# Activations in one tile per block of 512 tokens, and the last gate tiles block by block

## The chip, the cores and the metric

The kernel runs on one core of a Trainium2 chip. The metric is the time of one launch on the device in microseconds, here the median of three runs. Every matmul, vector operation and transfer that is named below belongs to that one core.

## The reference

Two layers of a hybrid encoder work on `x` of 2048 tokens and 1024 channels, in float32. What matters here:

```python
for l in range(DEPTH):                       # 2
    h = rms_norm(x, norm_w[l])
    proj = h @ w_in                          # q,k,v | z_a | decay, beta | conformer | gates
    q, k, v = silu(conv5(qkv)); q, k = l2_normalize(q), l2_normalize(k)
    o = delta_rule(q, k, v, g, beta) forwards + the same backwards, in chunks of tokens
    o = rms_norm per head(o) * dn_norm_w * silu(z_a)
    y_a = o @ w_dn_out
    u = silu(layer_norm(conv31(cf_val * sigmoid(cf_glu)))) * silu(z_b)
    y_b = u @ w_cf_out
    gate = sigmoid(gate_lg + gate_b)         # 2 x 1024 channels
    x = x + (gate[0] * y_a + gate[1] * y_b) @ w_out
return rms_norm(x, final_norm_w)
```

## The kernel before, in words

**Splits.** Each float32 operand of a dense product is split into a high part (`split`: a copy on ACT that rounds) and a low part (a subtraction on DVE). A dense product is three matmuls for every 128 input channels: high by high, high by low, low by high, each 128x512. In what follows a *unit* is three such matmuls. Weights come by `weight`: a load into `wraw` on SP's queue, then `whi` on ACT and `wlo` on DVE, with two buffers each.

**Stages of a layer.** First the projections, with conv, normalising and scalar work pumped in between. The last projection is the 16 tiles of gate logits (`gates`): half 0 (tokens 0 to 1023) runs there; half 1 is left as filling for the next stage. Then `delta`, 16 steps of the chunked delta rule, one chunk forwards (lane 0) and one backwards (lane 1) in each step. Then `merge`, which makes `y_a`, `y_b`, the gates and the product with `w_out`.

**One step of delta.** On TensorE: for both lanes `pk` (L971) and `pq` (L974), products of the keys and queries with the state; the next chunk's inverse is assembled in between by `prep` (L918, L928 and L931, L942 and L943, L951 and L952); `pw` (L987); `pn` and `po` (L996, L1005), the state's update and the output. From step 8 on a pair of chunks is ready in each step, and `finish` normalises it: squares on ACT (L1026), an rsqrt on DVE (L189 to L1040), scaling on ACT (L1044), transposes on TensorE (L1049), the product with `za` on DVE (L1050) and the store of `og`. These are short dependent pieces, so between them the program pulls filling: `pull(n)` takes n units from `filler`, and in each full step 5, 4, 4 and 4 of them. `pull` ends early at a `yield GAP`.

**The filling.** `filler` runs `gates(1)`, 32 products of 8 units, and then `early_merge`: it loads `u` of half 0 into the tile `uop`, splits it, and makes 16 products of 4 units into the tile `t1`. The order of PE, ACT, DVE and POOL in this stage is the written order (`bind`); SP's queue is ordered by a scheduler. The large tiles share four buffers. Activations `h` are kept as a high and a low tile per half, so half 1 holds two buffers up to the last unit of `gates(1)`; `uop` and `t1` need just these. So `early_merge` yields GAP eight times, four behind the loads and four with the splits: counted from 0, step 12 gets 12 units, 13 none and 14 eight, and what isn't pulled by the last step, 30 units, runs behind the last transposes. There, in `merge`, `og` is read back as `gop` and split, and its products with `w_dn` begin.

In `merge` the gate logits come back from memory as `gt` (L1206, a sigmoid on ACT), in buffers of the kind `hm`, five of them, which the rings of `delta` use too. `prep` loads the decay's rows as `gc` into the ring `rgb` (POOL adds a mask, L889, ACT takes the exponent, L895).

## Time and profile before

| | |
|---|---|
| median of 3 runs | 3243.44 us (3238.36 to 3246.26) |
| profiled execution | 3243.9 us |
| its span on the core | 3242.1 us |
| mean granted clock of TensorE | 0.986 |
| TensorE busy | 96 % |
| VectorE (DVE) busy | 74 % |
| ScalarE (ACT) busy | 43 % |
| GpSimd (POOL) busy | 9 % |

In the profile PE is TensorE, SP the queue that issues most transfers. A line such as L971 is one of the kernel before; in the changed kernel the same code stands four lines earlier in this stage (L967). A number in brackets is the time for which the engine stood idle ahead of the instruction, with what released it. The two layers have the same order; all rows are from the first, unless said.

### The profile page before, as it was taken

Reading aid. Unit: us, or ns where it says so; the run is one execution under the profiler, and the core shown is the slowest. Engines: PE = TensorE matmul, PEld = TensorE weight load, DVE = VectorE, ACT = ScalarE, POOL = GpSimd, SP = SyncE. Lnnn points to the kernel's source line nnn. Section 1 sums busy time; section 2 is a strip of 40 time slices with the busy share of each in tenths; the row PEclk is TensorE's granted clock in tenths of the full one; section 3 lists DMA queues with packets and bytes.
Section 4 is the critical chain, followed back from the end, with each engine's and each line's share of the span. In section 5 each row is a group of like instructions: output and inputs, shape, how many; then the busy total and the mean of one; then the engine's idle time right before and its main releaser. Section 6 shows DMA issues by size and latency. Waiting matters only on the chain. (4 is left out here: it accounts for less than half of the span.)

```text
span 3242.1 us, 51095 instructions
## 1 busy us (share of the span) xinstructions
PE 3110.2 (96%) x19110; PEld 2719.2 (84%) x19110; DVE 2392.3 (74%) x4401; ACT 1397.2 (43%) x3100; POOL 303.1 (9%) x297
## 2 busy tenths in 40 slices
PE   6999999999999998999999999999999999898998
PEld 5788888888878997787888888888887899887786
DVE  7689898997546687645676989898954567857655
ACT  5625152523344466533345242434234545655332
POOL 3000000000022231000000000000002122300000
PEclk9999999999999998999999999999999999999999
DMA  4323231324587786654413141313457777846634
GB/s 139 90 92 103 74 113 64 116 102 146 189 272 244 255 258 193 178 190 130 141 49 107 65 124 56 121 62 115 139 180 247 237 257 249 272 139 199 205 126 150
DMA packets 425879, 501.68 MB, mean 155 GB/s; under 512 B 95584, under 2 KB 260064, under 8 KB 425632
## 3 DMA queue, kind: packets, MB, share of 16 engines
q1 hardware_dynamic: 352880, 388.58, 38.6%
q10 hardware_dynamic: 64688, 80.09, 7.0%
q0 software_dynamic: 8064, 29.76, 2.4%
q8 instruction: 150, 2.46, 0.3%
q14 instruction: 97, 0.79, 0.1%
HBM read 342.74 MB, written 155.58 MB: 154 GB/s over the span
## 5 line engine op out<-in xcount | busy, mean ns | idle before, releaser
L173 PE MATMUL pd<-hhi,whi 128*128 128x512 f32 x2816 | 1093.8, 389 | 0.0
L175 PE MATMUL pd<-hhi,wlo 128*128 128x512 f32 x2816 | 1072.5, 381 | 2.0 <-DVE wlo L157 2.0
L174 PE MATMUL pd<-hlo,whi 128*128 128x512 f32 x2816 | 1073.2, 381 | 0.0
L734 DVE SCALAR_TENSOR_TENSOR cacc<-gp,vec,cacc 128x1009 f32<-128x1009 f32 (+1 forms) x480 | 614.2, 1280 | 38.0 <-ACT cacc L732 34.8
L173 PEld LDWEIGHTS pd<-hhi,whi 128*128 128x128 f32 x2816 | 535.6, 190 | 79.6 <-issue 1.2
L175 PEld LDWEIGHTS pd<-hhi,wlo 128*128 128x128 f32 x2816 | 535.1, 190 | 79.8 <-DVE wlo L157 3.6
L174 PEld LDWEIGHTS pd<-hlo,whi 128*128 128x128 f32 x2816 | 535.7, 190 | 73.1 <-issue 1.9
L156 ACT ACTIVATE whi<-wraw 128x512 fp32r<-128x512 f32 x400 | 242.9, 624 | 491.7 <-PE pd L174 337.0
L157 DVE TENSOR_TENSOR wlo<-wraw,whi 128x512 fp32r<-128x512 f32 x400 | 290.0, 738 | 217.6 <-ACT whi L156 207.9
L559 DVE SCALAR_TENSOR_TENSOR acc<-cin,vec,acc 128x1022 f32<-128x1022 f32 (+1 forms) x192 | 246.5, 1298 | 14.6 <-ACT acc L557 13.4
L175 PE MATMUL pd<-yhi,wlo 128*128 128x512 f32 x512 | 195.4, 382 | 5.9 <-DVE wlo L157 5.7
L173 PE MATMUL pd<-yhi,whi 128*128 128x512 f32 x512 | 195.2, 381 | 3.0 <-ACT whi L156 2.7
L174 PE MATMUL pd<-ylo,whi 128*128 128x512 f32 x512 | 194.3, 379 | 1.7 <-DVE ylo L157 1.7
L812 ACT ACTIVATE go<-pd,vec 128x512 f32<-128x512 f32 x128 | 87.0, 680 | 132.0 <-PE pd L175 122.5
L889 POOL TENSOR_TENSOR dm<-dm,con 128x512 f32<-128x512 f32 x64 | 82.1, 1299 | 534.8 <-DMA dm<-gc 494.4
L535 ACT ACTIVATE cin<-pd 128x512 f32<-128x512 f32 x96 | 57.0, 593 | 154.1 <-PE pd L175 153.9
L175 PEld LDWEIGHTS pd<-yhi,wlo 128*128 128x128 f32 x512 | 96.7, 189 | 23.6 <-DVE wlo L157 10.3
L1206 ACT ACTIVATE gt<-gt 128x1024 f32<-128x1024 f32 x64 | 67.5, 1056 | 112.9 <-DMA gt<-gt 111.9
L173 PEld LDWEIGHTS pd<-yhi,whi 128*128 128x128 f32 x512 | 96.8, 189 | 19.5 <-ACT whi L156 5.6
L746 ACT ACTIVATE ao<-pd 128x512 f32<-128x512 f32 x64 | 38.3, 598 | 170.0 <-PE pd L175 169.9
L174 PEld LDWEIGHTS pd<-ylo,whi 128*128 128x128 f32 x512 | 96.8, 189 | 15.7 <-DVE ylo L157 2.3
L980 ACT ACTIVATE dm<-pz,eg 128x128 f32<-128x128 f32 x240 | 68.5, 368 | 95.8 <-PE pz L974 89.8
(289 smaller groups left out, 4851.9 us busy)
## 6 DMA issues: line engine op xcount, KB each, us to landing
wraw<-w_in SPq DMA_DIRECT2D x240, 256.0 KB, 3.1
gt<-go ACTq DMA_DIRECT2D x128, 256.0 KB, 3.4
dl<-gr SPq DMA_DIRECT2D x128, 256.0 KB, 4.9
dl<-kq SPq DMA_DIRECT2D x64, 512.0 KB, 5.6
dl<-kv SPq DMA_DIRECT2D x64, 512.0 KB, 5.2
gt<-gt SPq DMA_DIRECT2D x64, 512.0 KB, 4.9
wraw<-w_out SPq DMA_DIRECT2D x96, 256.0 KB, 3.1
kq<-acc SPq DMA_DIRECT2D x16, 1024.0 KB, 5.4
```

The source lines that it names most:

```text
L156: self.nc.scalar.activation(hi, src, AF.Copy)
L157: self.nc.vector.tensor_tensor(out=lo, in0=src, in1=hi.bitcast(F32), op=ALU.subtract)
L173: mm(ps, whi[:, k, :], xhi, start=k == 0, stop=False)
L174: mm(ps, whi[:, k, :], xlo, start=False, stop=False)
L175: mm(ps, wlo[:, k, :], xhi, start=False, stop=k == kk - 1)
L535: nc.scalar.activation(cut(t[:, o + b * NB:o + (b + 1) * NB]), sort(ps), AF.Copy)
L559: self.nc.vector.scalar_tensor_tensor(out=out, in0=t[:, k:k + n], scalar=wc(k), in1=out, op0=ALU.mult, op1=ALU.add)
L734: self.nc.vector.scalar_tensor_tensor(out=acc, in0=t[:, k:k + n], scalar=wc(k), in1=acc, op0=ALU.mult, op1=ALU.add)
L812: nc.scalar.activation(cut(o), sort(ps), AF.Identity, bias=self.vec[:, V_GB + j:V_GB + j + 1])
L889: nc.gpsimd.tensor_tensor(out=gb, in0=gb, in1=msk[:, None, :].to_broadcast([P, 4, P]), op=ALU.add)
L980: nc.scalar.activation(hv(o1)[:, hd, :], pq[:, hd, :], AF.Copy, scale=eg[:, hd:hd + 1])
L1206: nc.scalar.activation(gt, gt, AF.Sigmoid)
```

## The change

`h` becomes one tile per block of 512 tokens (`h0` to `h3`), high and low parts together. In half 1 of the gates the last two tiles, 14 and 15, run first for block 2 and then for block 3, so that block 2's tile is last read by unit 240 of 256. `uop` is allocated there, and loaded by eight transfers of 128x512 in place of four of 128x1024; the splits of its first 512 tokens are written at units 250 to 253 of the gates, those of the second 512 between the units of the first `uop` product. `t1` takes the buffer of block 3. The eight GAPs are gone. The ring `rgb` has four places in place of two, and with that uses up `hm` buffers which `gt` had: one early sigmoid of `gt`, with a table load ahead of it and one behind, is no longer in step 1. Steps 12, 13 and 14 get 17 units of filling each; the 31 that they take are the 30 behind the last transposes and one of the last step.

```diff
 GAP = 0
+SPLITS = [250, 251, 252, 253]
 LEAD = (8, 10, 6, 6, 6, 4)
...
     def normalise(self, half, xn, r, wcol):
         nc = self.nc
-        hi = self.big([P, KD, HALF], F32R, f"hhi{half}")
-        lo = self.big([P, KD, HALF], F32R, f"hlo{half}")
-        self.nh[half] = (hi, lo)
+        hs = [self.big([P, 2, KD, NB], F32R, f"h{2 * half + b}") for b in range(2)]
+        self.nh[2 * half:2 * half + 2] = hs
...
-                self.split(hi[:, k, sl], lo[:, k, sl], t)
+                self.split(hs[b][:, 0, k, :], hs[b][:, 1, k, :], t)
...
         for blk in range(4):
             half, b = divmod(blk, 2)
-            if b == 0:
-                self.h[half] = (self.big([P, KD, HALF], F32R, f"hhi{half}"),
-                                self.big([P, KD, HALF], F32R, f"hlo{half}"))
-            hi, lo = self.h[half]
-            sl = slice(b * NB, (b + 1) * NB)
+            self.h[blk] = self.big([P, 2, KD, NB], F32R, f"h{blk}")
+            hi, lo = self.h[blk][:, 0], self.h[blk][:, 1]
             src = [a["x"][k, :, blk * NB:(blk + 1) * NB] for k in range(KD)]
...
     def hx(self, blk):
-        half, b = divmod(blk, 2)
-        hi, lo = self.h[half]
-        sl = slice(b * NB, (b + 1) * NB)
-        return lambda k: (hi[:, k, sl], lo[:, k, sl])
+        h = self.h[blk]
+        return lambda k: (h[:, 0, k, :], h[:, 1, k, :])
...
     def gates(self, half):
         nc = self.nc
-        ahead = self.weight(self.a["w_in"][self.l, 28], KD)
-        for j in range(16):
-            w = ahead
-            if j < 15:
-                ahead = self.weight(self.a["w_in"][self.l, 29 + j], KD)
-            for b in range(2):
-                blk = 2 * half + b
-                ps = self.pd()
-                for more in self.dense_steps(ps, w, self.hx(blk), KD):
-                    if more:
-                        yield 1
-                if self.rate:
-                    self.follow()
-                    self.pump(self.rate)
-                o = self.st("go")
-                nc.scalar.activation(cut(o), sort(ps), AF.Identity, bias=self.vec[:, V_GB + j:V_GB + j + 1])
-                self.astore(self.gt_d[j, :, blk * NB:(blk + 1) * NB], o)
-                yield 1
+        seq = [(j, b) for j in range(16) for b in range(2)]
+        if half:
+            seq = seq[:28] + [(14, 0), (15, 0), (14, 1), (15, 1)]
+        ws = {}
+        for i, (j, b) in enumerate(seq):
+            for q, _ in seq[i:]:
+                if q not in ws and len({z for z, _ in seq[i:] if z in ws}) < 2:
+                    ws[q] = self.weight(self.a["w_in"][self.l, 28 + q], KD)
+            blk = 2 * half + b
+            ps = self.pd()
+            for more in self.dense_steps(ps, ws[j], self.hx(blk), KD):
+                if more:
+                    yield 1
+            if self.rate:
+                self.follow()
+                self.pump(self.rate)
+            o = self.st("go")
+            nc.scalar.activation(cut(o), sort(ps), AF.Identity, bias=self.vec[:, V_GB + j:V_GB + j + 1])
+            self.astore(self.gt_d[j, :, blk * NB:(blk + 1) * NB], o)
+            yield 1
...
-        rgb, ro1, rvn, ro, rza, rst, dp = (ring(NB, n) for n in (2, 2, 2, 5, 2, 2, 2))
+        rgb, ro1, rvn, ro, rza, rst, dp = (ring(NB, n) for n in (4, 2, 2, 5, 2, 2, 2))
...
     def filler(self):
-        yield from self.gates(1)
-        self.drain()
-        self.rate = 0.0
-        yield from self.early_merge()
-
-    def early_merge(self):
+        wcf = self.a["w_cf"][self.l]
+        u = None
+        for n, v in enumerate(self.gates(1)):
+            yield v
+            if n == 30 * KD - 1:
+                self.drain()
+                self.rate = 0.0
+                u = self.big([P, 8, HALF], F32R, "uop")
+                raw = lambda k, b: u[:, 4 + k, b * NB:(b + 1) * NB]
+                for b in range(2):
+                    for k in range(4):
+                        self.load(raw(k, b).bitcast(F32), self.u_d[k, :, b * NB:(b + 1) * NB])
+            if n == 31 * KD - 1:
+                ahead = self.weight(wcf[0], 4)
+            if n in SPLITS:
+                k = SPLITS.index(n)
+                self.split(u[:, k, 0:NB], raw(k, 0), raw(k, 0).bitcast(F32))
+        self.u0 = u
+        self.t1 = self.big([P, KD, HALF], F32, "t1")
+        yield from self.early_merge(wcf, ahead, raw)
+
+    def early_merge(self, wcf, ahead, raw):
         nc = self.nc
-        self.t1 = self.big([P, KD, HALF], F32, "t1")
-        self.u0, load, split = self.operand_parts(self.u_d, 0, "uop")
-        for k in range(4):
-            load(k)
-        for _ in range(4):
-            yield GAP
-        ahead = self.weight(self.a["w_cf"][self.l, 0], 4)
-        for k in range(4):
-            split(k)
-            yield GAP
         for j in range(KD):
             wc = ahead
             if j + 1 < KD:
-                ahead = self.weight(self.a["w_cf"][self.l, j + 1], 4)
+                ahead = self.weight(wcf[j + 1], 4)
             for b in range(2):
                 sl = slice(b * NB, (b + 1) * NB)
                 ps = self.pd()
-                for more in self.dense_steps(ps, wc, lambda k: (self.u0[:, k, sl], self.u0[:, 4 + k, sl]), 4):
+                for k, more in enumerate(self.dense_steps(ps, wc, lambda k: (self.u0[:, k, sl], self.u0[:, 4 + k, sl]), 4)):
+                    if j == 0 and b == 0:
+                        self.split(self.u0[:, k, NB:HALF], raw(k, 1), raw(k, 1).bitcast(F32))
                     if more:
                         yield 1
                 nc.scalar.activation(cut(self.t1[:, j, sl]), sort(ps), AF.Copy)
```

On ACT, the end of step 12. `junk,oss` are the squares of `finish`, `go` a gate product's eviction, `eg` belongs to the next step's `pq`. Before:

```order
L1026 ACTIVATE junk,oss<-dm_6983 128x128
L1026 ACTIVATE junk,oss<-dm_6983 128x128 [waits Activation_49] x3
L1026 ACTIVATE junk,oss<-dm_6984 128x128 [waits Activation_49] x4
L812 ACTIVATE go<-pd,vec 128x512 [waits DMAHW7_49,PE_49]
L150 DMA gt_151<-go 128x512 [waits DMAHW5_49,Activation_49]
L980 ACTIVATE dm_6982<-pz,eg 128x128 [waits PE_49,Pool_49]
L980 ACTIVATE dm_6982<-pz,eg 128x128 x3
```

and now (`t` is the first eviction of a `uop` product):

```order
L1022 ACTIVATE junk,oss<-dh_6985 128x128 [waits Activation_49] x4
L157 ACTIVATE uop<-uop 128x512 [waits DMAHW2_49]
L157 ACTIVATE uop<-uop 128x512 [waits DMAHW6_49]
L808 ACTIVATE go<-pd,vec 128x512 [waits PE_49]
L151 DMA gt_150<-go 128x512 [waits DMAHW0_49,Activation_49]
L157 ACTIVATE whi<-wraw 128x512 [waits DMAHW7_49]
L157 ACTIVATE uop<-uop 128x512 [waits DMAHW7_49]
L157 ACTIVATE uop<-uop 128x512
L157 ACTIVATE uop<-uop 128x512 [waits DMAHW1_49]
L157 ACTIVATE uop<-uop 128x512 [waits DMAHW2_49]
L1163 ACTIVATE t_10818<-pd 128x512 [waits PE_49]
L976 ACTIVATE dm_6983<-pz,eg 128x128 [waits PE_49,Pool_49]
```

Two splits of `uop` now stand between the squares (the last four are shown) and `go`, and a `whi` and four more splits ahead of `t` and the next step's L976 (L980 before).

On TensorE, behind the last step. `con` is the identity of the transposes. Before:

```order
L1049 MATMUL pz<-con,dm_6984 128x128 x8
L173 MATMUL pd<-uop,whi 128x512
L174 MATMUL pd<-uop,whi 128x512
L175 MATMUL pd<-uop,wlo 128x512
L173 MATMUL pd<-uop,whi 128x512
```

and now:

```order
L1045 MATMUL pz<-con,dm_6984 128x128 [waits Activation_49] x8
L174 MATMUL pd<-gop,whi 128x512 [waits PE_49,Activation_49]
L174 MATMUL pd<-gop,whi 128x512 [waits PE_49]
L175 MATMUL pd<-gop,whi 128x512 [waits DVE_49]
L176 MATMUL pd<-gop,wlo 128x512
L174 MATMUL pd<-gop,whi 128x512 [waits Activation_49]
L175 MATMUL pd<-gop,whi 128x512
L175 MATMUL pd<-gop,whi 128x512 [waits DVE_49]
L176 MATMUL pd<-gop,wlo 128x512
```

The `uop` products behind the last transposes have left; the `gop` products of both blocks stand there, block by block as the splits come.

On SP, ahead of the first step: `gr`, `kq` and `kv` are a chunk's inputs, `w_in` the gates' weights. Before:

```order
L144 DMA dl_6981<-gr_142 128x4x128 x4
L144 DMA dl_6980<-kq_140 128x1024
L144 DMA dl_6980<-kv_141 128x1024
L144 DMA dl_6980<-kq_140 128x1024
L144 DMA dl_6980<-kv_141 128x1024
L144 DMA dl_6981<-gr_142 128x4x128 x4
L144 DMA dm_6982<-gc_144 128x512 x2
L144 DMA wraw<-w_in 128x512 x2
```

and now:

```order
L145 DMA dm_6982<-gc_143 128x512 x2
L145 DMA wraw<-w_in 128x512 x4
L145 DMA dl_6981<-gr_141 128x4x128 x7
L145 DMA dl_6980<-kq_139 128x1024
L145 DMA dl_6980<-kv_140 128x1024
L145 DMA dl_6980<-kq_139 128x1024
L145 DMA dl_6980<-kv_140 128x1024
L145 DMA dl_6981<-gr_141 128x4x128
L145 DMA wraw<-w_in 128x512 x2
```

The second pair of `gc` has gone ahead of the `gr` loads, and `w_in` follows them directly.

## Rows read from the trace of the kernel before

**Rows 1.** The page's first part: busy time, share, instructions.

```profile
PE 3110.2 (96%) x19110; PEld 2719.2 (84%) x19110; DVE 2392.3 (74%) x4401; ACT 1397.2 (43%) x3100; POOL 303.1 (9%) x297
```

**Rows 2.** Timeline of TensorE, starts of steps: start, us, engine, line, op, tiles, count.

```profile
1179.96 1.05 PE L971 MATMUL pz<-dh,dl 128*128 128x128 f32 x8
...
1203.72 1.05 PE L971 MATMUL pz<-dh,dl 128*128 128x128 f32 x8
...
1204.61 1.06 PE L974 MATMUL pz<-dh,dl 128*128 128x128 f32 x8
...
1224.13 1.16 PE L971 MATMUL pz<-dh,dl 128*128 128x128 f32 x8
...
1269.14 1.05 PE L971 MATMUL pz<-dh,dl 128*128 128x128 f32 x8
```

**Rows 3.** Stretches: length; PE, PEld, DVE, ACT, POOL busy; clock; DMA share; GB/s.

```profile
1199.00:1224.00 25.00, 25.00 (x275) 22.64 (x273) 21.11 (x55) 15.57 (x57) 6.97 (x6) 1.00 0.83 256
1224.00:1240.00 16.00, 14.05 (x194) 12.99 (x191) 15.40 (x44) 11.22 (x38) 5.88 (x5) 0.89 0.95 329
```

**Rows 4.** Timeline of TensorE, steps 13 and 14; idle and releaser in brackets.

```profile
1248.56 2.07 PE L971 MATMUL pz<-dh,dl 128*128 128x128 f32 x8 [5.97 <-DVE dm L1050]
...
1260.44 1.13 PE L1005 MATMUL pz<-dm,dl 128*128 128x128 f32 x8 [1.90 <-DVE dh L934]
...
1275.48 2.08 PE L971 MATMUL pz<-dh,dl 128*128 128x128 f32 x8 [4.39 <-DVE dm L1050]
```

**Rows 5.** Timelines of ACT (two rows) and DVE (one), prices and a wait.

```profile
1225.71 0.67 ACT L812 ACTIVATE go<-pd,vec 128x512 f32<-128x512 f32 x1
...
1266.68 1.28 ACT L1206 ACT_TABLE_LOAD   x1 [4.00 <-DMA gt<-gt]
...
1303.38 0.69 DVE L157 TENSOR_TENSOR wlo<-wraw,whi 128x512 fp32r<-128x512 f32 x1 [3.52 <-ACT whi L156]
```

**Rows 6.** Timelines of PE, ACT, DVE and SP, from the last output products on.

```profile
1287.44 1.95 PE L1005 MATMUL pz<-dm,dl 128*128 128x128 f32 x16
...
1291.64 0.31 ACT L1026 ACTIVATE junk<-dm 128x128 bf16<-128x128 f32 x1 [2.04 <-DVE dm L1007]
...
1296.60 0.69 DVE L157 TENSOR_TENSOR wlo<-wraw,whi 128x512 fp32r<-128x512 f32 x1 [2.73 <-ACT whi L156]
...
1299.90 2.45 ACT L1044 ACTIVATE dm<-dm,orr 128x128 f32<-128x128 f32 x8 [1.87 <-DVE orr L1040]
...
1301.12 1.62 PE L1049 MATMUL pz<-con,dm 128*128 128x128 f32 x8
...
1304.77 0.38 SPq L147 DMA_DIRECT2D og<-dm  x1
```

**Rows 7.** Timelines of SP, DVE and PE: the reload of `og`, the `gop` blocks.

```profile
1307.63 2.00 SPq L144 DMA_DIRECT2D gop<-og  x4
...
1316.88 2.36 DVE L157 TENSOR_TENSOR gop<-gop 128x1024 fp32r<-128x1024 f32 x2
...
1322.00 0.38 PE L173 MATMUL pd<-gop,whi 128*128 128x512 f32 x1
...
1324.59 0.38 PE L173 MATMUL pd<-gop,whi 128*128 128x512 f32 x1
```

**Rows 8.** Start of the stage: timelines of PE, ACT, SP, and one stretch.

```profile
913.61 0.28 PE L928 MATMUL pz<-dh,dh 32*32 32x32 f32 x4 [6.26 <-ACT dh L921]
...
912.01 1.38 ACT L156 ACTIVATE whi<-wraw 128x512 fp32r<-128x512 f32 x2 [8.84 <-DMA wraw<-w_in]
...
903.94 2.44 SPq L144 DMA_DIRECT2D dm<-gc  x2
...
900.00:920.00 20.00, 13.74 (x128) 11.13 (x127) 9.51 (x21) 8.80 (x26) 5.49 (x4) 0.83 0.99 309
```

**Rows 9.** Timeline of TensorE in step 1, first and second layer.

```profile
975.96 0.45 PE L918 MATMUL pz<-dh,dl 32*32 32x32 f32 x32 [1.30 <-DVE dl L954]
...
2555.74 0.45 PE L918 MATMUL pz<-dh,dl 32*32 32x32 f32 x32 [0.55 <-DVE dl L954]
```

More of the change, by code (lines that the diff above doesn't have):

```diff
@@ L277, in run @@
             self.ready = 0
-            h = [None, None]
+            h = [None] * 4
             self.h = h
@@ L331, in first_norm @@
                                                op0=ALU.mult, op1=ALU.mult)
-                nc.scalar.activation(hi[:, k, sl], x[k], AF.Copy)
-                nc.vector.tensor_tensor(out=lo[:, k, sl], in0=x[k], in1=hi[:, k, sl].bitcast(F32), op=ALU.subtract)
+                self.split(hi[:, k, :], lo[:, k, :], x[k])
                 if k == KD - 1:
@@ L1187, in merge @@
             self.load(nvec, a["vecs"][l + 1])
-        self.nh = [None, None]
+        self.nh = [None] * 4
         prev = None
```

## The prediction

> **What bounds the kernel now.** I read the page's busy times first, then the delta stage in stretches, then TensorE's own timeline, and last the chains that run while TensorE waits. TensorE is busy 3110.2 us of the span [rows 1], so only stretches in which it stands still, or runs at its lower clock, can be shortened. A full step of the delta stage takes 23.76 us from one first-lane L971 to the next (1179.96 to 1203.72), and the window 1199:1224 has TensorE busy all the time at clock 1.00 [rows 2, 3]. Step 13 starts at 1224.13 and step 15 at 1269.14, so steps 13 and 14 took 45.01 us [rows 2], though the order gives them 8 units of filling (a unit is three 128x512 matmuls; twelve take 2.59, from 1322.00 to 1324.59 [rows 7], so a unit 0.648) where full steps would have 34. The window 1224:1240 has 14.05 of 16 us busy at clock 0.89 [rows 3]. The idles: 5.97 and 4.39 us ahead of lane 1's L971, both behind DVE's L1050, and twice 1.9 ahead of L1005, behind DVE's L934 (the later stands) [rows 4]. Behind each long idle the clock is low: eight L971 took 2.07 us, where a full step's took 1.05 [rows 2, 4]. In these steps the chain prep, lanes, finish is the bound; in the others TensorE is. Then 30 units run after the last transposes and cover the stores of `og`, their reload and the splits of `gop`: the last split ends at 1319.24 and the first `gop` matmul starts at 1322.00 without idle [rows 7]. So the pause costs time in steps 13 to 15, but its leftover work is the cover of the tail. That is the question of this change.
>
> **The change, part by part.** Working per layer, from the first layer's rows; the second has the same order. I count from 1203.72 (step 12) to the end of the second `gop` block. The first ends at 1324.59, the second 2.59 later, so before it is 1327.18: 123.46 us.
>
> *The filling moves.* 31 units go into steps 12 to 14, 30 of them from behind the last transposes. Steps 12, 13 and 14 become full: 3 x 23.75 = 71.25. DVE is busy 21.11 of 25 us and ACT 15.57 in such a step [rows 3], so the extra evictions of `t` lie beside TensorE's work.
>
> *New wait at the first `uop` block.* The splits of block 0 stand on ACT behind the eight squares of step 12, two ahead of them and two behind, then come `go`, one `whi`, and block 1's first split. Before, the squares end and `go` starts at 1225.71 [rows 5]. From there ACT has five operations of 128x512, at 0.6 each (no `uop` row has that shape; `go` has it, 0.67 with some overlap), so it is done about 1228.7; DVE's half of the last split is 0.69 [rows 5], so 1229.4. Two of the unit's three matmuls follow, 0.43 us, and step 13 begins at 1229.9 to 1230.1, against 1203.72 + 23.75 = 1227.47: a stall of 2.65. Behind ACT's and DVE's waiting instructions stand L976 and L972 of step 13, which TensorE needs only after five more units. Its bounds: 0, if the squares come earlier now, and 6, if the loads land late. For the clock behind it I add 1.0, one group of L971 at the lower level [rows 4]. Together 71.25 + 3.65 = 74.9, against 65.42 before.
>
> *Step 15.* Before: 1269.14 to 1289.39, the end of the last output products [rows 2, 6], 20.25 us, with 4.39 idle and about 2 of slow clock. That idle came since ACT stood 4.00 us at the load of the table for `gt`'s sigmoid, with squares and a `whi` behind it, and DVE's `wlo` and L1050 behind that [rows 5]. Now the squares come ahead of the sigmoid, and nothing that the transposes need stands behind it but one `wlo`. The work alone is 13.0: four groups of eight at 0.89 (1203.72 to 1204.61 [rows 2]), nine units, and twice sixteen at 1.78. I leave 1.2 of wait (one table load is 1.28 [rows 5]) and 1.0 of clock: 15.2. Bounds 13.0 and 19.5.
>
> *The tail.* The chain is: L1007, squares on ACT (1291.64), `wlo`, the rsqrt steps, L1044 (1299.90), transposes (1301.12), a `wlo`, L1050, store at 1304.77 [rows 5, 6], 15.4 us behind 1289.39. Now one `wlo` no longer stands ahead of the last L1050 and the gates' product L1213 not ahead of L1007: 12.5. Bounds: 9.1 (if as much goes as DVE's two waits for `whi`, 2.73 and 3.52 [rows 5, 6]) and 15.4. Store to reload stays 2.9 (1304.77 to 1307.63). Reload to last split was 11.6 (to 1319.24) [rows 7]; one `t` eviction and one `whi` fewer lie between the splits: 10.6. Now nothing covers this. TensorE has no work from the last transposes until the first `gop` split, some 10 us. The order lets it take both blocks as the splits come, so about 1.0 is left after the last one, plus 2.1 for matmuls at 1.2 instead of 2.4 GHz (two groups' worth, as behind the 5.97 us of idle [rows 4]): 3.1. Some DVE work of the merge, which before ran under the filling, comes later: 0.7.
>
> Sum: 74.9 + 15.2 + 12.5 + 2.9 + 10.6 + 3.1 + 0.7 = 119.9, against 123.46. Gain 3.5 per layer. The pause loses some 21 us (steps 13 and 14 leave out 26 units, 16.8, and are only 2.5 shorter than two full ones: 14.3; step 15 takes 20.25 for work of 13.0: 7.2); the larger part is paid again at the end.
>
> The Trainium skill, page "TensorE: Matmul & The Clock Gate", section "HAM oscillation — how this bites in real kernels", says that a TensorE which waits for a DMA between bursts falls to half its clock and starts the next burst cold. The trace agrees behind DVE waits (2.07 against 1.05 [rows 4]); it speaks against putting one long idle ahead of `gop`. If all 24 matmuls of the two blocks ran cold, the 2.1 would be 5.2 and the gain 0.4 per layer.
>
> *The start of the stage.* TensorE stood 6.26 us at L928: ACT's zn copy stood behind two `whi`, which waited 8.84 for `w_in`, whose loads were queued on SP behind two `gc` loads of 2.44, issued at 903.94 after a ring of two came free [rows 8]. With a ring of four these `gc` loads go out earlier and `w_in` is ahead of 0.5 MB; at 309 GB/s, the rate of the window 900:920 [rows 8], that is 1.7 us. Bounds 0 (the transfers only change places) and 8.4 (the idle goes, and 2.1 of slow clock behind it). Gain 1.7.
>
> *One early sigmoid of `gt`* with its two table loads leaves step 1, since its buffer now belongs to the ring. Idle of 1.30 in the first layer and 0.55 in the second goes [rows 9]. The sigmoid itself comes later, beside other work.
>
> *At nothing:* tiles per block instead of per half, the same splits, eight loads and eight splits of 128x512 for `uop` instead of four of 128x1024 (ACT and DVE beside TensorE, in steps with the room named above; without it, the stall above grows).
>
> Total: 2 x 3.5 + 2 x 1.7 + 1.85 = 12.3 us. The profiled execution took 3243.9, the median is 3243.44; the difference goes on the median: 3243.44 - 12.3 = 3231.2, about **3231**.
>
> **The rivals.**
> *No stall at all.* DVE and ACT have room (21.11 and 15.57 of 25 us [rows 3]), so the splits could be done in time. Then 3.65 and the 2.2 of step 15 go: 5.85 per layer, 11.7 in all, 3219.5. Against it: ACT's order, in which two splits stand behind the squares.
> *All is given back.* The tail's chain stays at 15.4 (2.9 more) and the `gop` blocks run cold (3.1 more): a gain of -2.5 per layer, 3243.44 + 5.0 - 3.4 - 1.85 = 3243. For it: the chain's steps are latencies that no filling shortens. Against it: two rows of DVE's order have left it.
> *Slower: the `uop` loads on SP.* They stand, eight of them, in step 11 ahead of `o`, `za`, `gc`, `inv` and `kq` of the next step, and wait there for the last matmul of gate unit 240. DMA is 0.83 busy in 1199:1224 [rows 3]: 20.8 us of 25. Another 2.1 MB at 329 GB/s (window 1224:1240) is 6.4 us, so 2.2 more than fits. If `inv` or `kq` come late, both preps in flight and the lanes stall in steps 12 and 13. One such backlog of 2.2 is too little; it decides from 12.3 + 9.7 = 22 us over two layers, 11 in each, say twice 5.5 in steps 12 and 13. At 14 in each layer it is 3243.44 - 12.3 + 28 = 3259. Against it: such loads are issued about a step ahead.
> *It doesn't do what it says:* the `uop` tile still waits and the filling stands. Then about 3243. Against it: the order has no step without filling.
>
> **How the numbers follow.** What a measurement of this kernel can tell from no change is about 0.3%, 9.7 us: faster is under 3233.7. The forecast has 0.45 (3226 to 3237; 0.38 of it under the bound), no stall 0.20, given back 0.24, slower 0.07, not as it says 0.04. Faster 0.58, same 0.35, slower 0.07. The range 3219 to 3243 leaves out the slower cases and a part of the given-back ones above.
>
> **What would show it.** Right: L967 (L971 before) 23.75 us apart through step 14 and clock 1.00 there; a stall of 2 to 4 us at the first `uop` matmuls behind ACT or DVE; an idle of 8 to 12 us between the last transposes and the first `gop` matmul, released by ACT's `gop`; an idle at the start of the stage of about 4.5; no sigmoid in step 1. Wrong: idle behind DMA in steps 12 to 14 (the slower rival), a tail from the last output product to the store of `og` still over 15 us (given back), or a step 13 that starts at 23.75 (no stall).

## The result, and the profile after

The changed kernel takes 3220.63 us (median of six runs, 3214.18 to 3226.65); the kernel before took 3242.45 beside it. The ratio is 0.9932 with a 95% interval of 0.9917 to 0.9948: 21.8 us faster, where 12.3 were forecast. One execution of the kernel of experiment 7 took 4610.99 us at a mean granted clock of 0.712; it counts in the median given there (3220.39) but in no ratio. The profiled execution of the changed kernel took 3223.96 us. The first part of its page, span and busy times, answers to [rows 1]:

```profile
span 3222.2 us, 51090 instructions
PE 3101.0 (96%) x19110; PEld 2711.5 (84%) x19110; DVE 2401.9 (75%) x4409; ACT 1393.5 (43%) x3104; POOL 302.2 (9%) x297
```

To find where the time went, cut each layer's delta stage at four marks that both traces have: the first product of the first inverse (L918 before, L914 now), the first L971 (now L967) of step 1, the same of step 12, and the end of the second `gop` block. Differences of these marks, in us, first and second layer:

| stretch | before | after | gain | forecast gain |
|---|---|---|---|---|
| first inverse to step 1 | 45.09, 43.53 | 36.40, 36.41 | 8.69, 7.12 | 1.7, 1.7 |
| steps 1 to 11 | 255.82, 254.93 | 254.30, 254.30 | 1.52, 0.63 | 1.30, 0.55 |
| step 12 to second `gop` block | 123.46, 123.50 | 123.45, 122.51 | 0.01, 0.99 | 3.5, 3.5 |

The gain of these two executions is 15.8 us at the start of the stage and 1.0 us in the place that the change is about. With 2.2 in steps 1 to 11 that makes 19.0; what lies outside the marks adds the rest of the 19.9 by which the span is shorter: 1.1 lost ahead of the first layer's marks, 2.3 lost between those of the two layers, and 4.4 gained behind the last one.

**The end of the stage.** TensorE's timeline of the changed kernel, first layer: starts of steps 12 to 15, the first `uop` product, the following group, the last output products and the first `gop` matmul (idle and releaser in brackets); it answers to [rows 2, 4, 6, 7].

```profile
1194.63 1.05 PE L967 MATMUL pz<-dh,dl 128*128 128x128 f32 x8
...
1220.03 0.80 PE L174 MATMUL pd<-uop,whi 128*128 128x512 f32 x1 [3.42 <-ACT uop L157]
...
1224.07 0.63 PE L176 MATMUL pd<-uop,wlo 128*128 128x512 f32 x1
1224.49 1.92 PE L967 MATMUL pz<-dh,dl 128*128 128x128 f32 x8
...
1249.17 1.05 PE L967 MATMUL pz<-dh,dl 128*128 128x128 f32 x8
...
1272.93 1.05 PE L967 MATMUL pz<-dh,dl 128*128 128x128 f32 x8
...
1285.15 2.05 PE L1001 MATMUL pz<-dm,dl 128*128 128x128 f32 x16
...
1310.09 1.22 PE L174 MATMUL pd<-gop,whi 128*128 128x512 f32 x2 [9.88 <-ACT gop L157]
```

Steps 13 and 14 are full now: 24.68 (1224.49 to 1249.17) and 23.76. The idles of [rows 4] behind the transposes' products are gone, but for 0.74 in step 15. In their place stand the forecast ones: 3.42 us at the first `uop` product behind ACT, and 9.88 us ahead of `gop` behind ACT. The stretches of this kernel (length; PE, PEld, DVE, ACT, POOL busy; clock; DMA share; GB/s) show what the first costs beyond itself; they answer to [rows 3, 8].

```profile
900.00:920.00 20.00, 20.00 (x193) 16.55 (x192) 14.72 (x24) 12.14 (x33) 7.67 (x6) 1.00 1.08 373
1194.00:1216.00 22.00, 22.00 (x244) 20.07 (x243) 13.60 (x48) 12.17 (x36) 7.33 (x6) 1.00 1.05 347
1216.00:1229.00 13.00, 9.58 (x44) 7.57 (x42) 10.70 (x22) 9.17 (x30) 0.32 (x1) 0.74 0.68 216
1229.00:1249.00 20.00, 20.00 (x221) 17.91 (x220) 16.08 (x45) 15.08 (x50) 4.23 (x4) 1.00 0.53 167
...
1220.00:1226.00 6.00, 5.97 (x17) 4.42 (x18) 5.12 (x9) 4.26 (x8) 0.00 (x0) 0.50 0.49 159
1310.00:1315.00 5.00, 4.87 (x11) 3.43 (x12) 4.79 (x4) 4.02 (x5) 0.00 (x0) 0.50 0.86 338
```

The clock is 1.00 in the stretches around the stall and 0.74 in the 13 us with it; in 1220:1226 it is 0.50, the lower of its two levels. Nine `uop` matmuls behind the stall took 4.46 us (1220.03 to 1224.49), where nine at full clock take 1.94 (twelve take 2.59 [rows 7]). Six of the nine are followed by the next after 0.42 or 0.43 us, twice the 0.216 of full clock; the other three, after 0.59 to 0.72, which is some 0.6 us more in all. Behind the idle ahead of `gop` the clock is 0.50 as well (1310:1315).

**The start of the stage** is the first stretch above: before, 13.74 of 20 us busy at clock 0.83 [rows 8], now all 20 at 1.00. To see why, follow SP's queue. Timeline of SP in the kernel before, from the first chunk's inputs to the weights that ACT waits for:

```profile
891.04 2.69 SPq L144 DMA_DIRECT2D dl<-gr  x4
...
898.28 3.21 SPq L144 DMA_DIRECT2D dl<-gr  x4
903.94 2.44 SPq L144 DMA_DIRECT2D dm<-gc  x2
906.43 0.91 SPq L144 DMA_DIRECT2D wraw<-w_in  x2
```

The same of the changed kernel:

```profile
887.19 5.77 SPq L145 DMA_DIRECT2D dl<-gr  x7
...
896.50 0.52 SPq L145 DMA_DIRECT2D dl<-gr  x1
897.36 2.16 SPq L145 DMA_DIRECT2D wraw<-w_in  x2
...
904.62 0.32 SPq L145 DMA_DIRECT2D dm<-gc  x1
```

`w_in` leaves at 897.36 and not at 906.43, and on ACT's timeline the two `whi` wait 0.95 us where they waited 8.84 [rows 8]; the zn copy (L917) follows at once:

```profile
905.25 1.34 ACT L157 ACTIVATE whi<-wraw 128x512 fp32r<-128x512 f32 x2 [0.95 <-DMA wraw<-w_in]
906.49 0.26 ACT L917 ACTIVATE dh<-pz 128x128 f32<-128x128 f32 x1
```

A little over half of this shift is a wait at the head of that queue. SP's own waits in 870 to 912 us (us in total, times, longest), the row behind PE, kernel before:

```profile
SPq L144 <- PE pd L175: 7.6, 1, 7.6
```

and the changed kernel:

```profile
SPq L145 <- PE pd L176: 2.5, 1, 2.5
```

It is the wait ahead of the first `gr`. The buffers that the stage's inputs take are those of half 0's activations. Before, the high and the low tile are both read up to the very last product of `gates(0)`. With a tile per block, block 0's is last read by the product before, 8 units earlier, and 8 x 0.648 is 5.2 us: the 5.1 by which the wait is shorter. That is a reading of two traces in which three things differ (the ring, the blocks, the filling); the experiments take them apart. The new tile is no smaller than the old: 2 x 8 x 512 elements in each partition against 8 x 1024. What differs is which tokens share a tile.

### The profile page after: what moved, and what is told of

Same layout as the page of the kernel before. It is cut to its first block, busy times and chain, and to the rows that moved or that the text cites. A ratio compares the mean times of both kernels' runs of the same rounds, so it can differ in the third digit from the quotient of the medians.

```text
span 3222.2 us, 51090 instructions
## 1 busy us (share of the span) xinstructions
PE 3101.0 (96%) x19110; PEld 2711.5 (84%) x19110; DVE 2401.9 (75%) x4409; ACT 1393.5 (43%) x3104; POOL 302.2 (9%) x297
## 5 line engine op out<-in xcount | busy, mean ns | idle before, releaser
L174 PE MATMUL pd<-h,whi 128*128 128x512 f32 x2816 | 1091.7, 388 | 0.0
L176 PE MATMUL pd<-h,wlo 128*128 128x512 f32 x2816 | 1071.3, 380 | 2.3 <-DVE wlo L158 2.3
L175 PE MATMUL pd<-h,whi 128*128 128x512 f32 x2816 | 1072.1, 381 | 0.0
L174 PEld LDWEIGHTS pd<-h,whi 128*128 128x128 f32 x2816 | 534.6, 190 | 79.3 <-issue 1.4
L176 PEld LDWEIGHTS pd<-h,wlo 128*128 128x128 f32 x2816 | 534.4, 190 | 79.5 <-DVE wlo L158 3.9
L175 PEld LDWEIGHTS pd<-h,whi 128*128 128x128 f32 x2816 | 534.5, 190 | 72.9 <-issue 1.9
L158 DVE TENSOR_TENSOR wlo<-wraw,whi 128x512 fp32r<-128x512 f32 x400 | 279.7, 713 | 175.8 <-ACT whi L157 163.9
L174 PE MATMUL pd<-gop,whi 128*128 128x512 f32 x256 | 99.9, 392 | 20.5 <-ACT gop L157 19.3
L174 PE MATMUL pd<-uop,whi 128*128 128x512 f32 x256 | 102.9, 402 | 12.8 <-ACT uop L157 7.1
L976 ACT ACTIVATE dm<-pz,eg 128x128 f32<-128x128 f32 x240 | 68.5, 368 | 98.8 <-PE pz L970 93.7
```

The source lines that it names most:

```text
L158: self.nc.vector.tensor_tensor(out=lo, in0=src, in1=hi.bitcast(F32), op=ALU.subtract)
L174: mm(ps, whi[:, k, :], xhi, start=k == 0, stop=False)
L175: mm(ps, whi[:, k, :], xlo, start=False, stop=False)
L176: mm(ps, wlo[:, k, :], xhi, start=False, stop=k == kk - 1)
L976: nc.scalar.activation(hv(o1)[:, hd, :], pq[:, hd, :], AF.Copy, scale=eg[:, hd:hd + 1])
```

## The experiments

Each run's median and ratio stand against the kernel before on the same chip, with the 95% interval. The marks are those of the table above.

**1. The ring alone.** The kernel before with one edit:

```diff
-        rgb, ro1, rvn, ro, rza, rst, dp = (ring(NB, n) for n in (2, 2, 2, 5, 2, 2, 2))
+        rgb, ro1, rvn, ro, rza, rst, dp = (ring(NB, n) for n in (4, 2, 2, 5, 2, 2, 2))
```

> The kernel before with one number changed: the ring for gc has four places instead of two. Filling, GAPs and uop as before. Theory A (the gain is in the ring): in the changed kernel step 1 began 7.6 us earlier in the first layer and 7.1 in the second, and steps 1 to 3 gave 1.5 and 0.6 more, 16.8 in all, while steps 12 to 15 and the tail together gave -0.6 and +0.4. Then this kernel takes about 3242.5 - 16.8 = 3225.7 (ratio 0.9948), the idle of 6.26 at L928 is gone, and the idles of 5.97, 4.39 and twice 1.9 in steps 13 to 15 are still there. Theory B (the gain is in the filling that no longer pauses): the start of the stage differs by 1.7 per layer as I had priced it, and this kernel takes 3236 to 3240.

Measured: 3237.44, ratio 0.9982 (0.9973 to 0.9991), 5.9 us. The theory that the ring brings the whole gain at the start falls. TensorE still stands at L928, and SP still waits for half 0's last product, though `w_in` now leaves ahead of `gc`; TensorE, SP's wait, SP's timeline:

```profile
905.19 0.27 PE L928 MATMUL pz<-dh,dh 32*32 32x32 f32 x4 [3.86 <-ACT dh L921]
```

```profile
SPq L144 <- PE pd L175: 7.7, 1, 7.7
```

```profile
897.95 0.88 SPq L144 DMA_DIRECT2D wraw<-w_in  x2
899.00 1.04 SPq L144 DMA_DIRECT2D dm<-gc  x1
```

The start gains 2.06 and 1.68 us in the two layers, steps 1 to 11 gain 1.53 and 0.64: for the ring, the prediction's terms (1.7, and 1.30 and 0.55) were right. So `w_in` ahead of `gc`, with the long wait still ahead of both, gives these 2 us of the start and not the 8.69 and 7.12.

**2. The changed kernel with a ring of two.**

```diff
-        rgb, ro1, rvn, ro, rza, rst, dp = (ring(NB, n) for n in (4, 2, 2, 5, 2, 2, 2))
+        rgb, ro1, rvn, ro, rza, rst, dp = (ring(NB, n) for n in (2, 2, 2, 5, 2, 2, 2))
```

> The changed kernel with one number taken back: the ring for gc has two places again. The filling runs through steps 12 to 14 as in the change. Theory A: the idle of about 6 us at L924 is back, and the sigmoid in step 1; the pause's removal is worth -0.6 and +0.4 us by the two layers' marks, so the time is 3238 to 3242.5 (ratio 0.998 to 1.0). Theory B: 3222 to 3228.

Measured: 3229.10, ratio 0.9958 (0.9945 to 0.9971). Theory A falls; the time is 1 us above the range of theory B, which is tested by itself in experiment 5. The start is nearly as short without the ring (37.43 and 36.56), so something else makes it short. What came back is step 1's idle, 1.30 us in this trace as in [rows 9]:

```profile
962.15 0.45 PE L914 MATMUL pz<-dh,dl 32*32 32x32 f32 x32 [1.30 <-DVE dl L950]
```

**3. Tiles per block in half 0 alone.** The kernel before, where only half 0 takes the new tiles; half 1, the filling, its GAPs and the ring stay:

```diff
+    def halves(self, half):
+        if half == 1:
+            hi = self.big([P, KD, HALF], F32R, f"hhi{half}")
+            lo = self.big([P, KD, HALF], F32R, f"hlo{half}")
+            return [(hi[:, :, b * NB:(b + 1) * NB], lo[:, :, b * NB:(b + 1) * NB]) for b in range(2)]
+        hs = [self.big([P, 2, KD, NB], F32R, f"h{2 * half + b}") for b in range(2)]
+        return [(h[:, 0], h[:, 1]) for h in hs]
...
-        hi = self.big([P, KD, HALF], F32R, f"hhi{half}")
-        lo = self.big([P, KD, HALF], F32R, f"hlo{half}")
-        self.nh[half] = (hi, lo)
+        hs = self.halves(half)
+        self.nh[half] = hs
...
```

> The kernel before with one part of the change: the activations of tokens 0 to 1023 are held in one tile per block of 512; those of half 1 stay as they were, as do the filling with its GAPs, uop and the ring of two. Theory C (the start of the delta stage gains by the tiles per block): the stage's inputs go into the buffers of half 0's activations, and SP waited 7.6 us for the last gate product of half 0 before its first gr load in the kernel before, 2.5 us in the changed kernel, since the tile of block 0 comes free one product of 5.2 us earlier. Then from the first L918 to step 1 it takes 36.4 to 37.6 us here instead of 45.1 and 43.5, and the whole kernel is 14 to 16 us faster, 3227 to 3229 (ratio 0.9955), with all idles of steps 13 to 15 still there. Rival: the tiles alone don't move it and the ring is needed as well: 43 us or more, 3236 to 3243.

Measured: 3226.35, ratio 0.9952 (0.9939 to 0.9964), a little more than expected: 17.2 us by the medians and 15.6 by the ratio, from a part that the prediction had put at nothing. The start is 36.87 and 36.40, and the stage's end is what it was: 123.41 and 123.67, with the long idles still in it. The wait is short, and `w_in` leaves ahead of `gc` though the ring has two places; SP's wait behind PE, then its timeline:

```profile
SPq L144 <- PE pd L175: 2.4, 1, 2.4
```

```profile
882.47 5.36 SPq L144 DMA_DIRECT2D dl<-gr  x7
...
892.46 2.04 SPq L144 DMA_DIRECT2D wraw<-w_in  x2
...
899.86 0.99 SPq L144 DMA_DIRECT2D dm<-gc  x2
```

**4. All of the change but that.** The changed kernel, in which half 0 keeps its high and low tile (the function of experiment 3 with the halves exchanged):

```diff
     def normalise(self, half, xn, r, wcol):
         nc = self.nc
-        hs = [self.big([P, 2, KD, NB], F32R, f"h{2 * half + b}") for b in range(2)]
+        hs = self.halves(half)
         self.nh[2 * half:2 * half + 2] = hs
...
```

> The changed kernel with that same part taken back: the activations of tokens 0 to 1023 in a high and a low tile for all 1024, half 1 still per block, the ring of four, the filling that runs through. Theory C: the idle at L924 (its counterpart stands three lines lower here) is back at about 4 us, as with the ring of four alone, the way from the first z1 product to step 1 is 42 to 43 us, and the time is 3231 to 3236. Rival (the pause's removal makes the gain): 3219 to 3224.

Measured: 3231.43, ratio 0.9962 (0.9948 to 0.9976). This is what theory C expected. Taken out of the whole change the part is worth some 10 us (0.9962 against 0.9932), where by itself it was worth 15.6; the two agree within their intervals. The start is 43.25 and 41.68 again, as with the ring alone, and the idle is back, at about the length that it has with the ring alone:

```profile
912.17 0.28 PE L933 MATMUL pz<-dh,dh 32*32 32x32 f32 x4 [3.73 <-ACT dh L926]
```

SP's wait for half 0's products is 7.6 to 7.8 us in both layers of the four kernels with two tiles for half 0 (before, experiments 1, 4 and 5), and 2.3 to 2.5 in both layers of the changed kernel and of experiment 3.

**5. The pause alone.** Experiment 4 with a ring of two, so that only the new filling, which no longer pauses, is left.

```diff
-        rgb, ro1, rvn, ro, rza, rst, dp = (ring(NB, n) for n in (4, 2, 2, 5, 2, 2, 2))
+        rgb, ro1, rvn, ro, rza, rst, dp = (ring(NB, n) for n in (2, 2, 2, 5, 2, 2, 2))
```

> The change's filling alone: gate tiles of half 1 block by block, uop loaded early, no GAPs; the activations of tokens 0 to 1023 in two tiles for all 1024 as before, and the ring of two. Nothing is left out. My forecast for this part was 7 us (3.5 per layer). By the marks so far, from step 12 to the second gop block, it gives between -2 and +2.6 per layer, and the last merge was 2 to 5 us shorter in all kernels that have it. So I expect 3236 to 3242 (ratio 0.998 to 1.0 with 0.9985 the likeliest), the start of the stage as in the kernel before (43 to 45 us from the first z1 product to step 1). If the pause's removal is worth what its label says, some 21 us per layer of lost filling: under 3225.

Measured: 3243.92 against 3241.43, ratio 1.0002 (0.9993 to 1.0012). The 7 us that the prediction gave this part fall, and the time is 2 us above the range expected here: the new filling by itself is worth nothing that can be measured. From step 12 to the second `gop` block it took 125.77 us in one layer and 120.82 in the other (123.46 and 123.50 before). Its four longest idles on TensorE there, first layer, at the start, two `uop` products and the first `gop` matmul:

```profile
912.85 0.28 PE L933 MATMUL pz<-dh,dh 32*32 32x32 f32 x4 [5.24 <-ACT dh L926]
...
1228.67 0.48 PE L174 MATMUL pd<-uop,whi 128*128 128x512 f32 x1 [3.42 <-ACT uop L157]
...
1234.24 0.80 PE L175 MATMUL pd<-uop,whi 128*128 128x512 f32 x1 [2.14 <-DVE uop L158]
...
1321.94 1.22 PE L174 MATMUL pd<-gop,whi 128*128 128x512 f32 x2 [9.52 <-ACT gop L157]
```

**6. Blocks in half 0 and the ring, without the new filling:** experiment 3 with the edit of experiment 1.

> The other two parts of the change together, without the filling: the activations of tokens 0 to 1023 per block of 512, and the ring of four; half 1, uop and the GAPs as before. Marks to be expected: 36.4 us from the first z1 product to step 1 in both layers, 254.3 from there to step 12 (against 255.8 and 254.9), 123.4 from step 12 to the second gop block. Time 18 us under the kernel before, 3224 to 3227 (ratio 0.9945), so that the whole change would have 2 to 6 us from the filling. If the tiles and the ring do nothing for each other: as with the tiles alone, 0.9952.

Measured: 3224.68, ratio 0.9943 (0.9929 to 0.9956), as expected. The start is 36.41 in both layers, as in the changed kernel. Its interval and that of the changed kernel (0.9917 to 0.9948) overlap: on top of these two, the filling adds about 0.001, some 3 us, or nothing.

The next four ask what took the filling's gain: the stall at `uop` and the uncovered tail.

**7. All eight splits under the gates.** The changed kernel, where the splits of both `uop` blocks stand at units 246 to 253:

```diff
-SPLITS = [250, 251, 252, 253]
+SPLITS = [246, 247, 248, 249, 250, 251, 252, 253]
...
-                k = SPLITS.index(n)
-                self.split(u[:, k, 0:NB], raw(k, 0), raw(k, 0).bitcast(F32))
+                b, k = divmod(SPLITS.index(n), 4)
+                self.split(u[:, k, b * NB:(b + 1) * NB], raw(k, b), raw(k, b).bitcast(F32))
...
-                    if j == 0 and b == 0:
-                        self.split(self.u0[:, k, NB:HALF], raw(k, 1), raw(k, 1).bitcast(F32))
```

> The changed kernel with all eight splits of uop written at gate units 246 to 253, six of them ahead of the squares of step 12 on ACT instead of two. If the squares ahead of the splits make the stall: the idle of 3.42 and 3.72 us at the first uop block goes or falls under 1 us, step 12 takes 24 to 25 us instead of 29.9, and the time falls by 5 to 6 us per layer, to about 3209 to 3212 (ratio 0.990). If the lanes then wait for ACT instead (z2's copy stands behind four more splits): step 12 still takes 27 us or more, 3218 to 3222.

Measured: 3220.39, ratio 0.9927 (0.9915 to 0.9940), the time of the changed kernel, where over 8 us less was expected. Step 12 became full (23.75), and step 13 took 31.04 and 30.63. The wait had moved to lane 1's L967; TensorE, then DVE:

```profile
1223.46 2.08 PE L967 MATMUL pz<-dh,dl 128*128 128x128 f32 x8 [4.66 <-DVE dh L1046]
```

```profile
1219.93 1.29 DVE L158 TENSOR_TENSOR uop<-uop 128x512 fp32r<-128x512 f32 x2 [1.38 <-ACT uop L157]
1222.05 0.69 DVE L158 TENSOR_TENSOR wlo<-wraw,whi 128x512 fp32r<-128x512 f32 x1 [0.83 <-ACT whi L157]
1222.66 1.40 DVE L1046 SCALAR_TENSOR_TENSOR dh<-pz,vec,dh 128x512 f32<-128x512 f32 x2
```

DVE's L1046, which lane 1 needs, stands in the written order behind the low halves of the last two splits and a `wlo`, and these wait for ACT, which comes to them behind the squares.

**8. Sixteen units kept for the tail.** The changed kernel, pulling 13 units a step from step 12 on:

```diff
 STEP = (5, 4, 4, 4)
+LESS = (4, 3, 3, 3)
+FROM = 12
...
-            pull(STEP[0])
+            pull((STEP if step < FROM else LESS)[0])
...
```

and so for the other three pulls.

> The changed kernel, but from step 12 on each step pulls 13 units instead of 17 (4, 3, 3, 3), so that 16 units, 10.4 us of matmuls, are left for behind the last transposes. Nothing is left out. In the changed kernel TensorE stands 9.88 and 9.45 us between the last transposes and the first gop matmul, runs at the lower clock behind it, and stands 3.42 and 3.72 at the first uop block of step 12. If the tail's lost cover is what takes the pause's gain back: the steps 12 to 15 stay full (a step with 13 units needs 21.2 us, and a step without filling took 16.4 in the kernel before, so the chain is not yet the bound), the idle ahead of gop shrinks to under 2 us, and the time falls by 9 to 12 us per layer, to 3197 to 3203 (ratio 0.986 to 0.988). If instead the chain is the bound of these steps: idle in steps 12 to 15, and 3215 to 3225.

Measured: 3206.90, ratio 0.9889 (0.9872 to 0.9905). The idle ahead of `gop` fell from 9.88 to 2.23 us, and in the second layer from 9.45 to none. From step 12 to the second `gop` block it took 121.24 and 115.76 us, 9.0 less in all than the changed kernel. The stall stayed, and with less filling ahead of it is longer. TensorE:

```profile
1215.02 0.48 PE L176 MATMUL pd<-uop,whi 128*128 128x512 f32 x1 [4.29 <-ACT uop L159]
...
1303.95 0.91 PE L176 MATMUL pd<-gop,whi 128*128 128x512 f32 x2 [2.23 <-ACT gop L159]
```

**9. Both, and the splits earlier still:** experiment 8, and splits ahead of the squares of step 12 (numbers 0 to 3 are those of the first `uop` block, 4 to 7 of the second).

```diff
-SPLITS = [250, 251, 252, 253]
+SPLITS = {243: (0,), 244: (1,), 245: (2,), 246: (3,), 247: (4, 5), 248: (6, 7)}
...
```

> 16 units held for the tail as in the run with 13 units a step, and all eight splits of uop written in the first two fillings of step 12 (units 243 to 248), so that none stands behind the squares. Nothing is left out. If the stall at the first uop block is the squares on ACT and what stands behind them on DVE: the idles of 4.29 and 1.44 (first layer) and 3.75 (second) go, step 12 takes 21 to 22 us instead of 26.7 and 26.2, and the time is 3195 to 3199 (ratio 0.985 to 0.9865). If the splits push the chain of step 12 on DVE instead (as with six early splits, where lane 1's L967 then stood 4.66 us behind L1046): 3203 to 3208.

Measured: 3200.91, ratio 0.9873 (0.9860 to 0.9887). Step 12 to the second `gop` block is 116.12 and 113.48, against 123.45 and 122.51 of the changed kernel. It is between the two expectations, as smaller waits came instead; TensorE, first layer:

```profile
1208.97 0.66 PE L1047 MATMUL pz<-con,dm 128*128 128x128 f32 x4 [1.48 <-DVE dh L997]
...
1216.00 1.68 PE L969 MATMUL pz<-dh,dl 128*128 128x128 f32 x8 [1.82 <-DVE dh L1048]
...
1298.23 1.11 PE L176 MATMUL pd<-gop,whi 128*128 128x512 f32 x2 [2.00 <-ACT gop L159]
```

**10. The same, with three splits of the second block behind the gates,** at the places that they have in the changed kernel:

```diff
-SPLITS = [250, 251, 252, 253]
+SPLITS = {243: (0,), 244: (1,), 245: (2,), 246: (3,), 247: (4,)}
...
-                    if j == 0 and b == 0:
+                    if j == 0 and b == 0 and k:
...
```

> As the run with 16 units held and early splits, but only block 0's splits and one of block 1's are written in step 12, the other three between the first uop units in step 13, so that DVE has less ahead of L997 in step 12. Nothing is left out. If the 1.48 and 1.82 us (first layer) and 2.33 (second) that TensorE stood behind DVE's L997 and L1048 came from the four splits ahead of L997: steps 12 and 13 take 21 to 23 us each, and the time is 2 to 5 us under that run's 3200.9, 3196 to 3199. If one wait takes another's place again: 3200 to 3204.

Measured: 3200.86, ratio 0.9871 (0.9854 to 0.9887), the same as experiment 9 and as the second expectation says. The wait ahead of lane 1's L969 is the same, in a step 13 of 26.01 and 26.97 us:

```profile
1215.57 1.87 PE L969 MATMUL pz<-dh,dl 128*128 128x128 f32 x8 [1.82 <-DVE dh L1048]
```

These two are the fastest versions found: the changed kernel, with part of the filling left to cover the tail and the splits ahead of the squares.

## Why the prediction was right, and where it was wrong

The time lies in the range and the sign is right; the reason given for most of the sum is not what gained the time. That the range holds it is in part luck: 7.0 of the 12.3 us forecast were put on the filling, which by itself gave nothing (experiment 5), and some 16 came from a part put at nothing.

**The step that failed** is "At nothing: tiles per block instead of per half". Experiment 3 makes it 17.2 us (15.6 by the ratio), most of the 21.8, and experiment 4, which takes it out, has the long start of the ring alone back. The prediction followed ACT's wait back to `w_in` and `w_in` back to the two `gc` loads ahead of it on SP, and stopped there. Further back on the same queue, ahead of the first `gr`, stood SP's wait of 7.6 us for the last product of half 0, and all of the stage's inputs, `gc` and `w_in` were queued behind that. The edit to the tiles of half 0 changes which product ends that wait; it was costed by its instructions, not by who waits for its buffers. The upper bound of 8.4 per layer at the start was well sized (8.69 and 7.12 measured): the whole idle and the slow clock behind it did go, by another edit than the ring. So the sign of an idle of about 4.5 at the start is not there: the window 900:920 is busy throughout.

The Trainium skill says (page "Perfetto Trace Analysis", section "Optimization Strategy") that a gap that repeats on the busiest engine can mean that there is no room for the next tile yet, by the count of buffers or the size of tiles. The trace agrees in the main: the gap, once in each layer, was 6.26 and 5.00 us at the same line, behind loads that waited for a tile's memory, and more buffers (experiment 1) shortened it. What removed it (experiment 3) was a tile no smaller than before, but with other tokens in it.

**The ring and the early sigmoid** were right: 1.7 forecast and 2.06 and 1.68 measured, 1.85 forecast and 1.53 + 0.64 measured, with the ring alone.

**The stage's end** had the right mechanisms, and the forecast gain of 3.5 per layer came out as 0.0 and 1.0, since the stall's term was too small:

| term, us | forecast | layer 1, 2 |
|---|---|---|
| steps 12 to 14 | 74.9 | 78.30, 78.09 |
| step 15 | 15.2 | 14.27, 14.02 |
| from there to the second `gop` block | 29.8 | 30.88, 30.40 |
| sum | 119.9 | 123.45, 122.51 |

Stall and clock were put at 3.65 over three full steps of 23.75; they are 7.05 in the first layer. The idle itself is near (2.65 forecast, 3.42 measured), by two errors against each other: ACT reaches the splits behind the squares 24.7 us into the step and not 22.0 (the exponent L903 waits for DVE ahead of the squares), but TensorE goes on after the first of them, not after five operations. What was mis-sized is the clock: 1.0 was allowed, one group of eight at the lower level, and 2.7 in step 12 and 0.9 in step 13 are what is left of these steps beyond 23.75 and the idle, some 0.6 of it in the three longer matmuls. The nine slow `uop` matmuls, 2.5 us by themselves, were not in the sum. ACT's timeline, the exponent and the splits:

```profile
1214.74 1.26 ACT L903 ACTIVATE dh<-dh 32x128 f32<-32x128 f32 x4 [2.79 <-DVE dh L895]
...
1219.36 1.13 ACT L157 ACTIVATE uop<-uop 128x512 fp32r<-128x512 f32 x2
```

In the tail the store of `og` came 13.37 us behind the last output products (12.5 forecast). DVE's L1046 waited 2.44 us for `za` in it, and 0.32 more ahead of the second store; the changed kernel's DVE, on which `gop`'s low halves follow:

```profile
1299.79 0.75 DVE L1046 SCALAR_TENSOR_TENSOR dh<-pz,vec,dh 128x512 f32<-128x512 f32 x1 [2.44 <-DMA dh<-za]
1300.87 0.75 DVE L1046 SCALAR_TENSOR_TENSOR dh<-pz,vec,dh 128x512 f32<-128x512 f32 x1 [0.32 <-DMA dh<-za]
...
1310.07 5.04 DVE L158 TENSOR_TENSOR gop<-gop 128x1024 fp32r<-128x1024 f32 x4 [7.86 <-ACT gop L157]
```

Store to reload took 2.62 (2.9 forecast), reload to last split 11.92 (10.6), and what was left behind it 2.97 (3.8). The idle of 9.88 lies within the forecast 8 to 12, and its gap was the one that the clock page of the Trainium skill spoke against ("TensorE: Matmul & The Clock Gate", "HAM oscillation — how this bites in real kernels"): the trace agrees that the burst behind it starts at half clock (0.50 in 1310:1315). Experiment 8, which covers most of the gap with 16 units, is 13.7 us faster than the changed kernel by the medians; its marks show 9.0 of that between step 12 and the second `gop` block.

**The rivals.** "No stall at all" gave 3219.5, next to the measured time, and is false: the stall is there, and larger than forecast. "All is given back" is what befell the filling (experiment 5), though only in part by its mechanism, since the tail was 13.4 and not 15.4 and more than the forecast went into stall and clock. The slower one, loads of `uop` that hold up SP, isn't seen: DMA share in 1194 to 1216 us was 1.05 at 347 GB/s, and TensorE has no idle behind DMA in steps 12 to 14. "It doesn't do what it says" is false by the marks of steps 13 and 14.

**What stays open.** The parts don't add up: the ring gains 5.9 us alone and the filling nothing, but both together (experiment 4) 12.1. By the marks of experiment 4, 3.7 of it is at the start and 2.2 in steps 1 to 11, as with the ring alone. Another 2.4 is from step 12 on, and the stretch from the last layer's `gop` blocks to the end of the span is 330.0 us in place of 335.1. That last stretch was 329.4 to 333.8 in profiles with the new filling and 334.8 to 337.7 in those without; no run tells what in it differs. Nor is it fully shown why, in experiment 5, the filling lost 2.3 us in the first layer and saved 2.7 in the second (and much the same in experiment 2, also with a ring of two: 125.53 and 120.93). Part of it is the `uop` product at 1234.24, which stood 2.14 us behind DVE's split where its counterpart in the second layer stood 0.44.

## What to carry to other kernels

Follow a late load back along its issuing queue to the first instruction there that waits, not only to the loads just ahead of it: everything behind that one moves with it. Before an edit to a tile's shape is costed at nothing, ask which tiles take its memory next and which instruction frees it; here one product earlier, 5.2 us in each of two layers, was worth some 16. Work that fills one hole and is the cover of another gains only by what is left over, so try splitting it: moving all 31 units gave nothing by itself, and leaving 16 at the end while the splits came earlier made the best version, 0.987 of the time before.

## What the runs showed of the hardware

An idle of 3.42 us on TensorE cost about as much again behind it, most of it in clock: the steps with it took 3.6 us beyond the idle and their work. The granted clock was 1.00 before the idle and 0.50 in the 6 us from 1220 on, though TensorE was busy in 5.97 of them, and matmuls that took 0.216 us each took 0.43. And a busy DMA alone need not cost TensorE anything: in the changed kernel's stretches of 1.05 and 1.08 DMA share, at 347 and 373 GB/s, TensorE was busy all the time at clock 1.00; what counted at the start of the stage was when the transfers left SP, and that hung on one wait of 7.6 us at the head of its queue.
